# Rounding weights in a casting transfer and forming their rests in an adding transfer

## The chip, the cores and the metric

The kernel runs on one core of a Trainium2 chip. The metric is the device time of one execution in microseconds. Times inside an execution are counted from the start of its profiled span.

## What is computed

One layer of a decoder step for 576 tokens: 512 of a prompt and 64 of eight sampled sequences (8 each), with 16 learned tokens ahead of the prompt in the recurrent and attention branches. An input projection feeds two branches, a state-space scan and a sparse attention. Their outputs go through two projections, are weighted by gates and added, and then come the two parts that this document is about, cut to their core:

```
merged = sigmoid(g_ssm) * (y_ssm @ w_ssm_proj) + sigmoid(g_attn) * (y_att @ w_attn_proj)
h  = h + merged @ w_out                                  # w_out: 1024 x 1024
u2 = rmsnorm(h, norm2_w)
h  = h + square(relu(u2 @ w_up)) @ w_down                # w_up: 1024 x 4096, w_down: 4096 x 1024
y  = rmsnorm(h, final_norm_w)
```

All arrays are float32.

## The kernel before

**Two-part numbers.** TensorE runs in a format of fewer mantissa bits (`float32r`, FR in the code). To keep precision, an operand x is held as two tiles: hi, which is x rounded to that format, and lo = x - hi, the rest. A product of two such operands is three matmuls: hi*hi, hi*lo and lo*hi. The 64 sample tokens put their own hi and lo side by side in one tile, so that for them two matmuls do the work of three.

**Weights.** `weights` (from L125 on) loads a raw weight tile of 128 x 1024 into `wr` (two buffers for the whole kernel) by transfers that SyncE (SP) issues, and `split` (L122, L123) makes the two parts: ScalarE (ACT) writes hi from raw (L122), VectorE (DVE) writes lo = raw - hi (L123). Most weights go to the tiles `wh` and `wl` (three buffers each). The weights of the output projection `w_out` and of the lower projection `w_down` are taken by rows through `row_weights` (L1089) and go to `dh` and `dl`, seven buffers each, in the pool `p4w`. There are 40 such tiles of 512 KB: 8 of `w_out` and 32 of `w_down`.

**The output projection.** The five token blocks are taken in the order 4, 0, 1, 2, 3; block 4 is the 64 sample tokens, whose operand tile also holds their rests. `add_product` multiplies one block by four weight tiles and adds the result to `h2`. For each of the two column halves (512 wide) it collects the products of the four weight tiles in one PSUM accumulator: 12 matmuls for a prompt block, 8 for block 4 (L1177). VectorE then adds the accumulator to `h2` (L1179). The 1024 rows of `w_out` are done in two halves, four weight tiles each. Accumulators come from the groups "s" and "a", three of each. Before the first of them, the attention projection (matmuls at L145 into the accumulators "w") is finished. After the second half the second norm follows: squares on ScalarE (L1113), a power on GpSimd (POOL, L155), a scaling on VectorE, and transposes on TensorE (L1135).

**The MLP.** The 4096 hidden columns are cut into eight blocks of 512. For block s, `ups` makes four up projections (matmuls at L145 into "a"), and `add_product` multiplies the result by the four `w_down` tiles of the block, here with the accumulators "s" alone. The loop runs one block ahead: the up projections of block s + 1 are traced before the lower projection of block s, and the `w_down` tiles of block s between them:

```
    for s in range(8):
        ws = [] if s < 7 else row_weights(a["w_down"][0], 512 * s, 4)
        nxt = ups(s + 1, ws) if s < 7 else None
```

At block 7 there is no up projection left: its lower projection follows that of block 6 directly. The final norm and the stores come last.

**Order.** The program is traced in the order of the code. The framework's planner then sets the order of instructions on each engine, by estimates of its own of when operands and buffers are ready, and puts in the semaphores. Work from further down the code is thus moved forward where an engine would be idle. Each engine executes its own list strictly in order: an instruction that waits holds up all that stand behind it on that engine, transfers that the engine issues included. A tile whose slot is still read waits for its last reader.

Of the kernel before, what the change touches and what calls it, by code (L numbers as in the profile page):

```python
# [9 lines left out]
FT = mybir.dt.float32  # L10
FR = mybir.dt.float32r
BF = mybir.dt.bfloat16
I32 = mybir.dt.int32
AF = mybir.ActivationFunctionType
OP = mybir.AluOpType
# [55 lines left out]
def body(ctx, tc, a, o):  # L71
    nc = tc.nc
    SB, PS, DR = bass.MemoryType.SB, bass.MemoryType.PSUM, bass.MemoryType.DRAM
    act, dve, pool, pe, sy = nc.scalar, nc.vector, nc.gpsimd, nc.tensor, nc.sync
# [33 lines left out]
    def flat(t):  # L108
        return t.rearrange("p a b -> p (a b)")
# [11 lines left out]
    def split(raw, hi, lo, lo_eng=None):  # L121
        act.activation(hi, raw, AF.Copy)  # L122
        (lo_eng or dve).tensor_tensor(lo, raw, hi.bitcast(FT), op=OP.subtract)  # L123

    def weights(parts, at=None, lo_eng=None):  # L125
        raw = wp.tile([128, 8, 128], FT, tag="wr", name="wr", bufs=WB[0])
        lo, hi = [(at[0] if at else wp).tile([128, 8, 128], FR, tag=n, name=n, bufs=at[2] if at else WB[1])
                  for n in (at[1] if at else ("wl", "wh"))]
        for sel, src in parts:
            sy.dma_start(sel(raw), src)  # L130
        split(raw, hi, lo, lo_eng)
        return hi, lo

    def block(src, r0, c0, kt=8):
# [2 lines left out]
    def whole(src, r0, c0):  # L137
        return weights([(lambda r: r, block(src, r0, c0))])
# [45 lines left out]
    for t in range(5):  # L184
        xt = p0.tile([128, D], FT, tag="xt", name="xt", bufs=5)
        load_x(t, xt)
        if t == 4:
            sy.dma_start(xt[64:80], meta)
        if t == 2:
            w0 = weights([(lambda r: r[:, :, 0:96], w_in[:, C_KI:C_KI + 96].rearrange("(k p) c -> p k c", p=128)),  # L190
                          (lambda r: r[:, :, 96:128], w_in[:, C_DT:C_DT + 32].rearrange("(k p) c -> p k c", p=128))], lo_eng=dve)
        if t == 0:
            sy.dma_start(cst[0], a["cst"][:, 0:KEPT])
            sy.dma_start(wrow, rows(a["norm1_w"], D))
        xts.append(xt)
    ssq = p0.tile([128, 5], FT, name="ssq1")
    rs = p0.tile([128, 5], FT, name="rs1")
    for t in range(5):
        n = 128 if t < 4 else 80
# [6 lines left out]
        for q in range(2):  # L206
            ps = mis()
            pv = ps.rearrange("p (k n) -> p k n", k=4)
            for i in range(4):
                k = 4 * q + i  # L210
                pe.transpose(pv[:, i, :n], xn[:n, 128 * k:128 * k + 128], idf[:n, :n])
            h_ = uh[:, 4 * q:4 * q + 4, 128 * t:128 * t + n]
            act.activation(h_, pv[:, :, :n], AF.Copy)
            dve.tensor_tensor(ul[:, 4 * q:4 * q + 4, 128 * t:128 * t + n], pv[:, :, :n], h_.bitcast(FT), op=OP.subtract)  # L214
    wq0 = weights([(lambda r: r, block(w_in, 0, C_QI))])

    cwr = p0.tile([128, 128], FT, name="cwr")
# [70 lines left out]
    with tc.tile_pool(name="p1", bufs=1) as p1:  # L288
# [76 lines left out]
        for b2 in range(2):  # L365
            for e in range(2):
                src = qis[64 * e:64 * e + 64].rearrange("p c (i b s) -> p b i c s", b=2, s=8)[:, b2]
# [49 lines left out]
        for t in range(4):  # L417
            at = am[:, LO[t]:LO[t] + LT[t]]
# [82 lines left out]
        for kt in range(6):  # L501
            c0, n = ((128 * kt, 128) if kt < 4 else (512, 16) if kt == 4 else (528, 64))
# [515 lines left out]
    for q in range(4):  # L1018
# [7 lines left out]
        for m in range(8):  # L1026
            if m % 2 == 0:
                src = w_s[512 * q:512 * q + 512, 128 * m:128 * m + 256].rearrange("(k p) c -> p k c", p=128)
# [29 lines left out]
    for m in range(8):  # L1058
        parts = []
        for e in range(2):  # L1060
            for hp in range(2):
                r0 = 64 * (8 * hp + 4 * e)
# [25 lines left out]

    def row_weights(src, r0, n, at=(p4w, ("dl", "dh"), 7)):  # L1089

        return [[flat(x) for x in weights([(flat, src[r0 + 128 * k:r0 + 128 * k + 128, :])], at)] for k in range(n)]

    wo = row_weights(a["w_out"][0], 0, 4)
    def norm_rows(name):
        row = p4.tile([128, D], FT, tag="wrow", name="wrow", bufs=1)
# [87 lines left out]
    for q in range(2):  # L1183
        ws = row_weights(a["w_out"][0], 512, 4) if q else wo
        for t in ORDER:
            add_product(t, [mgh[:, 4 * q + k, :] for k in range(4)], [mgl[:, 4 * q + k, :] for k in range(4)], ws, banks="sa")
            if q == 1:
                turns.append(norm2(t))
                if t in (0, 1, 2):
                    turns.pop(0)()  # L1190
# [15 lines left out]
    def ups(s, ws=None):  # L1206
        hh = [p5.tile([128, NQ + NS], FR, tag="hh", name="hh", bufs=9) for _ in range(4)]
        hl = [p5.tile([128, NP], FR, tag="hl", name="hl", bufs=9) for _ in range(4)]

        def w_up(f):  # L1210
            return whole(a["w_up"][0], 0, 512 * s + 128 * f)

        f0 = 0
        if s == 0:
            f0 = 3
            w3 = [w_up(f) for f in range(3)]
            for c in PARTS:
                for f in range(3):
                    up(w3[f], f, hh, hl, *c)
                    if turns:  # L1220
                        turns.pop(0)()
        for f in range(f0, 4):
            w = w_up(f)
            for c in HALVES:
                up(w, f, hh, hl, *c)
            if ws is not None:
                ws += row_weights(a["w_down"][0], 512 * (s - 1) + 128 * f, 1)
        return hh, hl
# [36 lines left out]
```

## Time and profile before

| | us |
|---|---|
| median of 3 runs (1493.74 to 1494.7) | 1494.07 |
| the profiled execution | 1499.61 |
| its span, first to last instruction | 1497.8 |
| TensorE busy | 1443.2 (96%) |
| VectorE busy | 973.9 (65%) |
| ScalarE busy | 695.1 (46%) |
| GpSimd busy | 324.1 (22%) |
| 40 rounding passes on `dh`, ScalarE | 42.5 |
| 40 subtractions into `dl`, VectorE | 49.0 |

The profiled execution is 5.5 us longer than the median of the runs without a profile. Busy time counts the instructions of an engine and not the issuing of transfers; the ends of matmuls are modelled, since they overlap. In a row of a timeline the first number is the start in us, the second the length. In a row of a tile the three numbers are the least, the median and the greatest length in ns, then come the first and the last start. "x40" is a count. "SPq" and "POOLq" are the queues of SyncE and GpSimd. What stands in brackets behind a row of a timeline is the idle time ahead of it on its engine and what ended it.

### The profile page before, as it was taken

How to read it: one execution, taken by the hardware profiler on the slowest of the kernel's cores; microseconds unless marked ns; L12 is line 12 of the kernel's file. 1: busy time of each engine (PE TensorE's matmuls, PEld its weight loads, DVE VectorE, ACT ScalarE, POOL GpSimd, SP SyncE). 2: the span in 40 equal slices, each digit the busy share in tenths (PEclk: the TensorE clock that was granted, in tenths of full speed). 3: DMA queues.
4: the chain of work that ended last, by engine and by line, in shares of the span. 5: the costliest groups of instructions: out<-in, count | busy, mean ns of one | idle time of the engine just before them, and what ended most of it. 6: DMA issues, size and time to landing. Idle time of an engine off the chain costs nothing.

```text
span 1497.8 us, 26553 instructions
## 1 busy us (share of the span) xinstructions
PE 1443.2 (96%) x9960; PEld 1293.7 (86%) x9960; DVE 973.9 (65%) x2010; ACT 695.1 (46%) x1548; POOL 324.1 (22%) x475
## 2 busy tenths in 40 slices
PE   6899999999999999999999999999999999999998
PEld 5899989987888888889688888898898998899886
DVE  5599989998868767582644777665654444444434
ACT  4454255546665654542655777732352331232211
POOL 1100011426636335342423633100000000000001
PEclk9899999999999999999999999999999999999999
DMA  6334365768897887878964532146143321231202
GB/s 178 107 66 118 115 173 167 208 195 220 231 263 201 255 221 197 247 198 252 293 228 142 155 87 79 43 129 194 50 133 93 99 85 57 85 112 58 84 28 70
DMA packets 297609, 221.54 MB, mean 148 GB/s; under 512 B 43821, under 2 KB 267361, under 8 KB 297457
## 3 DMA queue, kind: packets, MB, share of 16 engines
q1 hardware_dynamic: 292232, 200.98, 47.5%
q0 software_dynamic: 5248, 18.88, 3.7%
q8 instruction: 78, 1.28, 0.4%
q14 instruction: 51, 0.41, 0.1%
HBM read 174.97 MB, written 44.07 MB: 146 GB/s over the span
## 4 chain that ended last, share of the span: by engine, by line
PE 76%; DMA 11%; DVE 5%; ACT 2%; issue 2%; SPq 1%; POOL 1%; POOLq 0%; DVEq 0%; ACTq 0%
PE w L145 22%; PE s L1177 16%; PE a L145 14%; PE w L1039 7%; PE s L871 2%; PE a L1177 2%; PE s L1005 2%; DMA out_dram<-st 1%; DMA bc<-d_ac 1%; DMA wr<-in_w_ssm_proj_dram 1%; DMA st<-in_state_ssm_dram 1%; PE s L734 1%; PE a L894 1%; PE a L995 1%; DMA d_x<-tk 1%
## 5 line engine op out<-in xcount | busy, mean ns | idle before, releaser
L145 PE MATMUL w<-uh,wh 128*128 128x288 f32 (+1 forms) x1168 | 359.1, 307 | 12.8 <-DVE qS L322 4.3
L145 PE MATMUL w<-uh,wl 128*128 128x288 f32 (+1 forms) x1168 | 354.9, 304 | 0.0
L145 PE MATMUL w<-ul,wh 128*128 128x288 f32 (+1 forms) x1168 | 352.6, 302 | 0.6 <-DVE ul L214 0.6
L145 PEld LDWEIGHTS w<-uh,wh 128*128 128x128 f32 x1168 | 223.6, 191 | 20.5 <-issue 7.1
L123 DVE TENSOR_TENSOR wl<-wr,wh 128x1024 fp32r<-128x1024 f32 x129 | 161.1, 1249 | 117.1 <-ACT wh L122 114.9
L145 PEld LDWEIGHTS w<-ul,wh 128*128 128x128 f32 x1168 | 223.5, 191 | 3.9 <-issue 2.3
L145 PEld LDWEIGHTS w<-uh,wl 128*128 128x128 f32 x1168 | 222.4, 190 | 1.5 <-issue 0.8
L122 ACT ACTIVATE wh<-wr 128x1024 fp32r<-128x1024 f32 x129 | 136.3, 1056 | 147.5 <-PE w L145 84.5
L145 PE MATMUL a<-u2h,wh 128*128 128x288 f32 (+2 forms) x512 | 151.4, 296 | 0.0
L145 PE MATMUL a<-u2l,wh 128*128 128x288 f32 (+2 forms) x512 | 151.2, 295 | 0.0
L145 PE MATMUL a<-u2h,wl 128*128 128x288 f32 (+2 forms) x512 | 151.2, 295 | 0.0
L1177 PE MATMUL s<-dl,hh 128*128 128x512 f32 (+1 forms) x324 | 126.9, 392 | 0.0
L1177 PE MATMUL s<-dh,hh 128*128 128x512 f32 (+1 forms) x324 | 126.8, 392 | 0.0
L1179 DVE TENSOR_TENSOR h<-h,s 128x512 f32<-128x512 f32 (+1 forms) x91 | 61.2, 679 | 100.4 <-PE s L1177 100.3
L122 ACT ACTIVATE dh<-wr 128x1024 fp32r<-128x1024 f32 x40 | 42.5, 1062 | 178.1 <-PE s L1177 138.3
L155 POOL TENSOR_TENSOR rs<-rs,cst 128x1 f32<-128x1 f32 (+2 forms) x15 | 8.3, 552 | 446.0 <-DVE rs L154 445.9
L1177 PE MATMUL s<-dh,hl 128*128 128x512 f32 (+1 forms) x260 | 101.7, 391 | 0.0
L145 PEld LDWEIGHTS a<-u2l,wh 128*128 128x128 f32 x512 | 96.1, 188 | 0.6
L145 PEld LDWEIGHTS a<-u2h,wh 128*128 128x128 f32 x512 | 96.1, 188 | 0.6
L145 PEld LDWEIGHTS a<-u2h,wl 128*128 128x128 f32 x512 | 96.1, 188 | 0.0
L1039 PE MATMUL w<-ysh,wh 128*128 128x288 f32 x256 | 78.4, 308 | 0.2 <-DVE ms L1044 0.2
L123 DVE TENSOR_TENSOR dl<-wr,dh 128x1024 fp32r<-128x1024 f32 x40 | 49.0, 1225 | 45.3 <-ACT dh L122 45.2
(384 smaller groups left out, 3220.1 us busy)
## 6 DMA issues: line engine op xcount, KB each, us to landing
wr<-in_w_in_dram SPq DMA_DIRECT2D x64, 512.0 KB
wr<-in_w_up_dram SPq DMA_DIRECT2D x32, 512.0 KB
wr<-in_w_down_dram SPq DMA_DIRECT2D x32, 512.0 KB
st<-in_state_ssm_dram SPq DMA_DIRECT2D x16, 512.0 KB
bc<-d_ac SPq DMA_DIRECT2D x32, 256.0 KB
out_dram<-st SPq DMA_DIRECT2D x16, 512.0 KB
wr<-in_w_ssm_proj_dram SPq DMA_DIRECT2D x16, 512.0 KB
d_xd<-th SPq DMA_DIRECT2D x16, 296.0 KB
```

The source lines that it names most:

```text
L122: act.activation(hi, raw, AF.Copy)
L123: (lo_eng or dve).tensor_tensor(lo, raw, hi.bitcast(FT), op=OP.subtract)
L145: pe.matmul(ps[:, :c1 - c0], p[:, k, :], x[:, c0:c1], start=(k == 0 and i == 0), stop=(k == 7 and i == 2))
L155: pool.tensor_tensor(dst, dst, K("half")[:p, :cols], op=OP.pow)
L734: pe.matmul(py[64 * (hh % 2):64 * (hh % 2) + 64, 128 * (hh // 2):128 * (hh // 2) + n], xt[:n, 64 * hh:64 * hh + 64], mt, start=True, stop= ...
L871: pe.matmul(v[64 * hp:64 * hp + 64], QZ[:, hp, :], kk, start=True, stop=True)
L894: pe.matmul(py[h, 0:128], PTs[:, s, h], Vg[s // 4][:, 256 * (s % 4) + 128 * hp:256 * (s % 4) + 128 * hp + 128], start=(s == 0), stop=False)
L995: pe.transpose(pv[:, j, :], P2[:, e, 128 * j:128 * j + 128], idf)
L1005: pe.matmul(py[64 * e:64 * e + 64, 0:256], Vt[:, j, kv:kv + 64], PT[:, e, j], start=(j == 0), stop=False)
L1039: pe.matmul(ps[:, :HQ], p[:, k, mc], x[k][:, c0:c1], start=(k == 0 and i == 0), stop=(k == 3 and i == 2))
L1177: pe.matmul(ps, x, w[:, cc], start=(k == 0 and i == 0), stop=(k == len(ws) - 1 and i == len(terms) - 1))
L1179: dve.tensor_tensor(h2[:, t, cc], h2[:, t, cc], ps, op=OP.add)
```

## The change

For the 40 tiles of `dh` and `dl`, the raw tile, its load by SyncE and the subtraction on VectorE go. A new function takes their place:

```
+    def weights_by_dma(src, at, view):
+
+        lo, hi = [at[0].tile([128, 8, 128], FR, tag=n, name=n, bufs=at[2]) for n in at[1]]
+        pool.dma_start(out=view(hi), in_=src)
+        act.activation(lo, hi.bitcast(FT), AF.Copy, scale=-1.0)
+        pool.dma_start(out=view(lo), in_=src, accum_op=OP.add)
+        return hi, lo
...
     def row_weights(src, r0, n, at=(p4w, ("dl", "dh"), 7)):
 
-        return [[flat(x) for x in weights([(flat, src[r0 + 128 * k:r0 + 128 * k + 128, :])], at)] for k in range(n)]
+        return [[flat(x) for x in weights_by_dma(src[r0 + 128 * k:r0 + 128 * k + 128, :], at, flat)] for k in range(n)]
```

The first transfer reads the weights in float32 and writes hi in the format of TensorE. ScalarE writes -hi into lo. The second transfer reads the same weights again and adds them to lo, which then holds the weights less hi. GpSimd issues both transfers. The number of buffers, the matmuls and all other weights (`w_in`, `w_ssm_proj`, `w_attn_proj`, `w_up`) stay as they are.

## The prediction

> **What bounds the kernel now.** I read the page's head first, then a table of busy time by stage, then the chain that ended last, then the rows of the two tiles that the change rewrites.
>
> ```profile
> PE 1443.2 (96%) x9960; PEld 1293.7 (86%) x9960; DVE 973.9 (65%) x2010; ACT 695.1 (46%) x1548; POOL 324.1 (22%) x475
> ...
> PEclk9899999999999999999999999999999999999999
> ```
>
> ```profile
> core 0: us, PE busy (x) PEld busy (x) DVE busy (x) ACT busy (x) POOL busy (x), PEclk, DMA share, GB/s
> 975.00:1024.00 49.00, 49.00 (x357) 48.33 (x358) 32.09 (x62) 18.27 (x26) 0.47 (x1) 0.95 0.50 149
> 1024.00:1081.00 57.00, 57.00 (x283) 47.00 (x282) 32.96 (x50) 14.78 (x25) 4.21 (x7) 0.95 0.35 107
> ...
> 1128.00:1440.00 312.00, 312.00 (x1834) 281.02 (x1833) 140.34 (x234) 87.50 (x149) 0.00 (x0) 1.00 0.27 82
> 1440.00:1460.00 20.00, 20.00 (x87) 16.05 (x87) 5.93 (x10) 0.07 (x1) 0.00 (x0) 1.00 0.00 0
> ...
> 1488.00:1498.00 10.00, 2.85 (x25) 2.65 (x23) 4.90 (x9) 1.74 (x6) 3.66 (x5) 0.78 0.27 105
> ```
>
> ```profile
> 1128.36 6.52 PE s L1177 x28
> 1134.88 0.80 PE a L145 x6
> 1135.67 19.59 PE s L1177 x84
> 1155.26 24.80 PE a L145 x186
> ...
> 1438.60 49.47 PE s L1177 x212
> 1488.06 0.02 issue
> ```
>
> TensorE is busy in every microsecond of the stages that the change touches: 49.00 of 49.00, 57.00 of 57.00, 312.00 of 312.00. The chain says the same: from 1128.36 to 1488.06 it is matmuls and nothing else. One step of the loop over the hidden blocks is 6.52 + 0.80 + 19.59 + 24.80 = 51.7 us. A 512-wide matmul comes every 19.59 / 84 = 0.2333 us, and no stage in the chain shows a gap that a faster producer could close. VectorE and ScalarE are near half idle there (140.34 and 87.50 of 312.00), GpSimd and most of the DMA engines wholly or nearly so. So time can be lost in these stages, but hardly won.
>
> **What is removed.** The rows of tile dh and of its raw buffer wr:
>
> ```profile
> L122 ACT ACTIVATE dh<-wr x40: 1046/1062/1067, 1000.9 to 1462.4; 128x1024 fp32r<-128x1024 f32 x40
> L123 DVE TENSOR_TENSOR dl<-wr,dh x40: 1218/1225/1227, 1002.0 to 1463.5; 128x1024 fp32r<-128x1024 f32 x40
> L130 SPq DMA_DIRECT2D wr<-in_w_down_dram x32: 327/328/340, 1091.6 to 1425.6; - x32
> L130 SPq DMA_DIRECT2D wr<-in_w_out_dram x8: 327/328/339, 997.3 to 1021.9; - x8
> ```
>
> 40 subtractions of 1.225 us leave VectorE: 49.0 us of busy time. None lies on the chain, so the gain is 0. 40 issues of 0.33 us leave SyncE: 13 us, also off the chain, gain 0. ScalarE still passes over each tile once (now it writes the negated rounded tile instead of the rounded one), 40 x 1.062 us as before, change 0. The two-slot raw buffer wr now serves the up projection alone, so those loads start sooner. No matmul waits for them today, so that too is 0. What covers all of this is the full TensorE; it goes only if a new stall opens.
>
> **What is added.** Two GpSimd transfers for each of 40 tiles. No casting or adding transfer is in this trace. The nearest rows are the gathers that GpSimd issues, in 512 KB (Kg, Vg: 128 rows of 4 KB, as a weight tile has) and 256 KB (kr):
>
> ```profile
> L385 POOL DMA_INDIRECT kr<-in_cache_kidx_dram,idx x8: 942/978/1175, 35.3 to 109.8; - x8
> ...
> DMA to landing us min/median/max: 3.3/3.5/6.7
> ...
> L850 POOL DMA_INDIRECT Kg<-in_cache_k_dram,idx x16: 934/938/1761, 687.8 to 771.6; - x16
> ...
> DMA to landing us min/median/max: 4.4/6.3/15.9
> ...
> L850 POOL DMA_INDIRECT Vg<-in_cache_v_dram,idx x16: 932/937/1517, 690.4 to 805.8; - x16
> ...
> DMA to landing us min/median/max: 4.3/4.6/4.9
> ```
>
> Issue: 80 x 0.94 = 75 us of GpSimd, in some 500 us in which it does almost nothing. Hidden. Landing of the casting transfer: 4.3 to 6.3 us; I take 4.6 (Vg's median: where it counts, from 1440 on, the DMA engines are at 0.00). The adding transfer must also read the tile it adds to. kr against Vg gives (4.3 - 3.3) = 1.0 us for 256 KB more, so 512 KB more are 2.0 us: an estimate of 6.6 us, with 4.3 (the extra read is free) and 8.3 (Kg's median plus 2.0) as ends. Whether adding itself runs slower than copying, no row shows; that is a rival below.
>
> So the way from a free slot to a finished rest changes from 1.06 + 1.23 = 2.3 us (the raw tile lay waiting in wr) to 4.6 + 1.06 + 6.6 = 12.3 us. What counts is where this way is not started early enough. Seven slots serve dh and dl, four tiles make a step. The first three tiles of a step take slots free for a whole step; the fourth takes the slot of the first tile of the step before, free only in that step's last group of twelve matmuls. For the hidden blocks 0 to 6 the fourth tile then has the 24.80 us of up-projection matmuls ahead of it: slack 24.8 - 12.3 = 12 us, cost 0. Twice there is no such cover.
>
> **Place one, the last step (block 7).**
>
> ```profile
> 1392.52 33.41 SPq L130 DMA_DIRECT2D wr<-in_w_down_dram  x5
> ```
>
> ```profile
> 1462.42 1.06 ACT L122 ACTIVATE dh<-wr 128x1024 fp32r<-128x1024 f32 x1 [22.35 <-PE s L1177]
> ```
>
> ```profile
> 1461.99 0.40 PE L1177 MATMUL s<-dh,hl 128*128 128x512 f32 x1
> ...
> 1464.55 0.39 PE L1177 MATMUL s<-dh,hh 128*128 128x512 f32 x1
> ...
> 1466.18 0.40 PE L1177 MATMUL s<-dl,hh 128*128 128x512 f32 x1
> ```
>
> The last raw tile is issued by 1425.9 (1392.52 + 33.41) and lies ready; its split starts at 1462.42, right after the matmul that frees the slot (1461.99 + 0.40 = 1462.39). Step 7 begins at 1464.55, and its eighth matmul, at 1466.18, is the first to want the fourth rest. After the change the transfer can start only at 1462.39: rounded tile at 1467.0, negated at 1468.1, rest at 1474.7. What TensorE can do meanwhile: three accumulators of the group "s" can hold the first three weight tiles of token block 4 (two halves, 6 matmuls each) and of half a block 0 (9): 21 x 0.2333 = 4.9 us, then the four products with the rounded fourth tile, 0.9 us. That ends at 1470.4. Stall: 4.3 us. Ends: 1.7 us (4.3 + 1.06 + 4.3), and 7.7 us (6.3 + 1.06 + 8.3). If the order of TensorE stays as it is, the wait starts at 1466.18 and costs 8.5 us with the middle values. I take 4.3, because the order is written by a planner that fills such a wait, as the next rows show.
>
> **Place two, the second half of the output projection.**
>
> ```profile
> 1044.01 0.40 PE L1177 MATMUL s<-dh,mgl 128*128 128x512 f32 x1
> ...
> 1046.57 0.39 PE L1177 MATMUL a<-dh,mgh 128*128 128x512 f32 x1
> ...
> 1051.47 0.40 PE L1177 MATMUL s<-dl,mgh 128*128 128x512 f32 x1
> ```
>
> Eight tiles share seven slots; the eighth waits for the first, free at 1044.01 + 0.40 = 1044.41. In group "s" its rest is used at 1051.47. In plain order (8 matmuls in "a", then 8 in "s") that would be the sixteenth from 1046.57, at 1046.57 + 15 x 0.2333 = 1050.07: the planner put six other products in front. New finish: 1044.41 + 12.3 = 1056.7. Six accumulators are in use here ("s" and "a"), with room for 12 + 4 x 9 = 48 matmuls, 11.2 us, to 1057.8. Stall 0 with a full refill, 5.2 us with today's order (1056.7 - 1051.47); I take 0.6, as the planner's own figure for these transfers is not visible.
>
> **GpSimd's queue.** The adding transfer waits, at the head of GpSimd's queue, for ScalarE, which waits for the casting one. Behind it can stand the powers of the second norm:
>
> ```profile
> 1059.15 0.57 POOL L155 TENSOR_TENSOR rs<-rs,cst 64x1 f32<-64x1 f32 x1 [1.67 <-DVE rs L154]
> ```
>
> Five of them feed the token blocks that TensorE needs from 1064 on, and the first w_down tiles take their slots in just this stretch. One wait costs between 0 and 4.6 us; other matmuls cover most. I take 0.5. Sum: +4.3 + 0.6 + 0.5 = +5.4 us.
>
> The profiled execution took 1499.61 us with a span of 1497.8; the sum puts that span at 1503.2. The runs without the profile have a median of 1494.07, and a stall is the same there: 1494.07 + 5.4 = 1499.5 us.
>
> **Rule against row.** The Trainium skill, "DMA: Bandwidth & Descriptors", section "Anatomy of one DMA — SWDGE (gpsimd) path", prices a GpSimd transfer at 2.0 us plus its bytes at 436 GB/s: an estimate of 3.2 us for 512 KB, where this trace has 4.3 at the least. By it the last rest would be there at 1469.9 and the stall of place one would be zero. The same page's "Rules for kernel authors" says that an adding transfer reads its destination and writes it later; that speaks for a price above Vg's, but no run so far shows one.
>
> **Rivals.** *Hidden (not slower).* The planner sets other work before the fourth tile, or the landings are short. For: it did so at 1046 to 1051. Against: with the least landing of the rows, 4.3 us, and a full refill there is still 1.7 us of stall. It decides where the way from slot to rest falls under 1470.4 - 1462.4 = 8.0 us. Time: 1494 to 1496.5, say 1495. The page's 3.2 us is this case. Chance 0.27.
>
> *Order unchanged, or a slow adder.* The planner reckons the transfers too short: 8.5 + 5.2 + 0.5 = +14.2 us, 1508. An adding transfer of 12 us does about as much (+5.4 at each place). For: nothing here prices it. Chance 0.18.
>
> *The DMA engines become the bound from 975 to 1024.*
>
> ```profile
> 690.00:740.00 50.00, 46.48 (x333) 37.04 (x333) 20.88 (x43) 24.61 (x54) 15.68 (x16) 0.92 0.92 299
> ```
>
> Seven w_out tiles would move 1.0 to 1.5 MB each instead of 0.5: with 149 GB/s over 49 us that makes some 11 to 14.5 MB, 220 to 300 GB/s, as much as in the one stage that is full (0.92), where TensorE lost 50.00 - 46.48 = 3.5 us. Against: the loads can spread, and the attention weights are fetched a step ahead. +9 us with the stalls above, 1503. Chance 0.05.
>
> *Faster.* Less VectorE work might raise the granted clock of 0.95 before 1128. Against: at 0.95 a 512-wide matmul comes every (1046.57 - 1044.01) / 11 = 0.233 us, at 1.00 every 0.2333, so the clock is not what sets the pace, and over 3 us is hardly possible. 1490.5. Chance 0.03.
>
> **How the numbers follow.** The forecast (4 to 6 us of stall, 1497 to 1502) has 0.47. A measurement tells 0.2% from no change, 3.0 us here: 1491.1 to 1497.1. Hidden lies in it whole, and 0.05 of the forecast: same 0.32. Faster 0.03. Slower 0.42 + 0.18 + 0.05 = 0.65. The range takes in hidden, the order unchanged and a rather slow adder, 1493 to 1510; outside are the faster case and the worst adders, some 0.13.
>
> **What will show it.** Right: TensorE idle of 2 to 8 us between 1462 and 1478, put down to a DMA on dl or to ScalarE; GpSimd rows of some 0.94 us, 80 of them; landings of 4.5 us for dh and 6 to 7 for dl; VectorE 49 us less busy, SyncE without w_down. Wrong: TensorE full to the end (hidden), idle in each 51.7 us step (slow adder), or idle before 1024 (DMA). A rewritten order of the query stage before 975, since GpSimd and ScalarE have work there too, would make all of this beside the point.

## The result and the profile after

| | before | after |
|---|---|---|
| median | 1493.9 us (1492.65 to 1494.7, 4 runs) | 1513.76 us (1510.26 to 1519.93, 4 runs) |
| profiled execution, span | 1497.8 us | 1517.9 us |
| TensorE busy | 1443.2 us | 1446.8 us |
| VectorE busy | 973.9 us | 930.4 us |

The ratio of the runs is 1.0142, 95% interval 1.0112 to 1.0172; by the medians the change costs 19.9 us. The forecast was 1499.5 us, the range ended at 1510. The direction was right, the size was not. All line numbers from the new function on are 8 higher: the product is now at L1185, its addition to h2 at L1187, the norm's transposes at L1143; the casting transfer is L137, the negation L138, the adding transfer L139. In the experiments the numbers are up to four higher still.

The stages of the prediction's table, in the changed kernel. The columns are those shown there: the length of the stage, busy time and count of TensorE, weight loads, VectorE, ScalarE and GpSimd, granted clock, share of the DMA engines, GB/s.

```profile
975.00:1024.00 49.00, 42.40 (x279) 39.91 (x279) 20.27 (x44) 16.57 (x24) 6.38 (x8) 0.93 0.85 207
1024.00:1081.00 57.00, 52.92 (x273) 44.64 (x271) 25.66 (x45) 13.29 (x19) 8.69 (x12) 1.00 0.58 162
...
1128.00:1440.00 312.00, 312.00 (x1840) 281.28 (x1839) 112.51 (x205) 85.28 (x145) 33.86 (x48) 1.00 0.47 117
...
1460.00:1488.00 28.00, 25.14 (x108) 19.87 (x106) 5.26 (x8) 1.06 (x1) 1.41 (x2) 1.00 0.18 38
```

TensorE was full in all of these. Now it lacks 6.6 us in the first, 4.1 in the second, 2.9 in the last, while the long loop is as full as before, with VectorE down from 140.34 to 112.51. The changed kernel's waits of TensorE after 960 us give the places, with the sum, the count and the longest of each:

```profile
PE a L1185 <- issue: 5.4, 1, 5.4
PE s L1185 <- DMA dl<-in_w_down_dram: 3.1, 1, 3.1
PE w L1143 <- DVE xn L1131: 2.1, 1, 2.1
PE a L1143 <- DVE xn L1131: 2.0, 1, 2.0
PE w L153 <- DVE tga L1080: 1.2, 1, 1.2
```

**The burst, 968 to 1005 us.** Seven casting transfers leave GpSimd at 968.78 and 974.18, seven adding ones between 978.71 and 994.19. Busy time in slices of 10 us, first the changed kernel, then the kernel before:

```profile
970.00:980.00 10.00, 9.23 (x67) 7.96 (x66) 5.52 (x12) 4.83 (x8) 3.86 (x7) 1.00 1.07 367
980.00:990.00 10.00, 10.00 (x72) 9.70 (x71) 3.12 (x6) 5.63 (x7) 4.00 (x5) 1.00 1.06 226
990.00:1000.00 10.00, 8.23 (x55) 7.25 (x53) 2.11 (x5) 1.40 (x2) 0.87 (x1) 1.00 1.07 214
1000.00:1010.00 10.00, 5.16 (x14) 4.14 (x15) 5.34 (x11) 3.15 (x5) 0.00 (x0) 0.66 0.96 215
```

```profile
980.00:990.00 10.00, 10.00 (x77) 10.00 (x76) 5.76 (x13) 3.81 (x6) 0.00 (x0) 0.95 0.57 161
990.00:1000.00 10.00, 10.00 (x77) 10.00 (x76) 6.43 (x14) 2.50 (x5) 0.00 (x0) 0.95 0.45 130
```

The DMA engines are full for 40 us (a share a little above 1 stands for full). While the casting transfers run they move 367 GB/s, while the adding ones run about 215. In the same stretch SyncE has to bring the attention weights and the gate rows `tga`. It issues them as early as before; changed kernel first, then before:

```profile
979.57 0.49 SPq L1075 DMA_DIRECT2D tga<-d_g  x1
980.10 4.90 SPq L130 DMA_DIRECT2D wr<-in_w_attn_proj_dram  x3
...
985.92 19.00 SPq L130 DMA_DIRECT2D wr<-in_w_attn_proj_dram  x4
```

```profile
979.65 0.49 SPq L1067 DMA_DIRECT2D tga<-d_g  x1
980.18 4.90 SPq L130 DMA_DIRECT2D wr<-in_w_attn_proj_dram  x3
...
985.77 5.71 SPq L130 DMA_DIRECT2D wr<-in_w_attn_proj_dram  x4
```

But they land late. By the semaphore updates in the trace, the gate rows issued at 979.57 landed at 991.43 (before: 979.65 and 983.04), and the last piece of an attention tile, issued at 980.74, landed at 1001.84, after 21.1 us (before: 980.83 and 984.18, 3.4 us). The 19.00 us of the next four issues are a sign of the same: two of them take 3.82 and 5.46 us instead of 0.62 and 0.60, and the last one waits for the buffer that the late tile holds. TensorE waits for the late landings, not for these four issues. The timeline of the changed kernel shows who waits, in the bracket at the end of each row:

```profile
991.52 0.46 DVE L1080 SCALAR_TENSOR_TENSOR tga<-tga,w 128x288 f32<-128x288 f32 x1 [6.57 <-DMA tga<-d_g]
...
1001.99 1.06 ACT L122 ACTIVATE wh<-wr 128x1024 fp32r<-128x1024 f32 x1 [8.09 <-issue]
...
1004.84 0.76 PE L1185 MATMUL a<-dh,mgh 128*128 128x512 f32 x1 [5.45 <-issue]
```

VectorE waits 6.57 us for the gate rows. ScalarE waits 8.09 us for the late attention tile; its split stood at 988.54 before. The rounding of merged rows stands behind that split in ScalarE's list, so the next products with merged rows are late too. TensorE, which had brought w_out products forward meanwhile, runs dry at 999.39. After the restart at 1004.84 it has a granted clock of 0.50 until 1009, which is the 0.66 of the last slice.

**The second norm, 1076 to 1081 us.** Block 4 is the first to be normed, and its 64-row transfer into `other` comes before everything else:

```profile
1053.64 0.55 POOL L137 DMA_DIRECT2D dh<-in_w_out_dram  x1 [16.02 <-PE s L1185]
1054.34 0.54 POOL L137 DMA_DIRECT2D dh<-in_w_down_dram  x1
1055.04 0.53 POOL L137 DMA_DIRECT2D dh<-in_w_down_dram  x1 [0.16 <-PE s L1185]
1055.73 0.53 POOL L137 DMA_DIRECT2D dh<-in_w_down_dram  x1 [0.17 <-PE s L1185]
1058.98 0.89 POOL L139 DMA_DIRECT2D dl<-in_w_out_dram  x1 [2.72 <-ACT dl L138]
...
1069.19 0.52 SPq L1118 DMA_DIRECT2D other<-h  x1
1073.75 1.22 DVE L1119 TENSOR_TENSOR h<-h,other 64x1024 f32<-64x1024 f32 x1 [2.24 <-DMA other<-h]
...
1078.35 0.71 PE L1143 MATMUL w<-cst,xn 64*128 64x64 f32 x8 [2.15 <-DVE xn L1131]
```

The eighth w_out tile gets its slot at 1053.64, three w_down casting transfers go out before its adding one, and block 4 is done only near 1069. From there to the first transpose it is a serial chain of 9.2 us (1069.19 to 1078.35), and the products that TensorE had left for it ended at 1076.2. Behind the two waits the granted clock is 0.50 from 1081 to 1084. The three casting transfers did not hold up the adding one in GpSimd's queue: GpSimd was idle for 2.72 us ahead of it, until ScalarE had negated the tile.

**Block 7.** This is place one of the prediction:

```profile
1477.28 0.55 POOL L137 DMA_DIRECT2D dh<-in_w_down_dram  x1 [39.25 <-PE s L1185]
...
1481.26 1.06 ACT L138 ACTIVATE dl<-dh 128x1024 fp32r<-128x1024 f32 x1 [26.59 <-DMA dh<-in_w_down_dram]
...
1482.61 0.86 POOL L139 DMA_DIRECT2D dl<-in_w_down_dram  x1 [4.78 <-ACT dl L138]
...
1488.24 0.94 PE L1185 MATMUL s<-dl,hh 128*128 128x512 f32 x3 [3.11 <-DMA dl<-in_w_down_dram]
...
1491.12 0.63 PE L1185 MATMUL s<-dl,hh 128*128 128x512 f32 x1
1491.54 0.63 PE L1185 MATMUL s<-dh,hh 128*128 128x512 f32 x1
...
1493.94 0.40 PE L1185 MATMUL s<-dh,hh 128*128 128x512 f32 x1
1494.17 0.40 PE L1185 MATMUL s<-dh,hl 128*128 128x512 f32 x1
```

From the free slot to the first product with the rest it takes 11.0 us. TensorE has other work for 7.9 us of it (it runs dry at 1485.14). The last rows show a cost behind the stall: for eight matmuls the pitch is 0.42 us (1491.12 to 1491.54) instead of 0.23 (1493.94 to 1494.17), 1.5 us in all. It is the granted clock, which falls to 0.50 some 2 us after the restart:

```profile
1491.00:1492.00 1.00, 1.00 (x4) 0.71 (x4) 0.00 (x0) 0.00 (x0) 0.00 (x0) 0.50 0.81 176
```

**The account.** One number per stretch is less noisy than the whole time: O runs from the first matmul of the attention projection to the first one of the up projection, M from there to the last hi*hi one of the lower projection. Ahead of O even the old kernel differs from execution to execution: in two profiles of it, on one chip, O began at 934.1 and at 944.2 us, while O and M agreed within 0.3 us. All values in us, from the starts of those matmuls:

| kernel | O | M | time against its own before |
|---|---|---|---|
| before | 132.4 | 415.0 | |
| after | 146.5 | 420.5 | 1.0142 [1.0112, 1.0172] |
| e0, e9 all old | 131.5, 131.7 | 415.4, 415.1 | 1.0016 [0.9992, 1.0041], 1.0003 [0.998, 1.0025] |
| e1, e8 w_down only | 132.8, 139.0 | 420.4, 421.0 | 1.0111 [1.0092, 1.0129], 1.0074 [1.0049, 1.01] |
| e2 w_out only | 140.4 | 415.0 | 1.0106 [1.0083, 1.0129] |
| e3 second transfer copies | 136.9 | 417.2 | 1.0073 [1.0047, 1.01] |
| e4 two tiles old | 140.7 | 415.0 | 1.0105 [1.0081, 1.0129] |
| e5 31 w_down tiles only | 132.4 | 415.0 | 1.0026 [0.9999, 1.0052] |
| e6 paced | 150.0 | 421.5 | 1.0203 [1.0186, 1.022] |
| e7 paced, two tiles old | 145.1 | 415.2 | 1.0117 [1.0094, 1.014] |
| e10 eight slots | 139.9 | 415.1 | 1.0052 [1.0025, 1.008] |
| e11 three w_out tiles | 135.3 | 415.0 | 1.002 [0.9996, 1.0044] |
| e12 old, eight slots | 133.3 | 415.0 | 1.0016 [0.9995, 1.0038] |
| e13 w_down, eight slots | 132.5 | 415.1 | 1.0014 [0.9991, 1.0037] |
| e14 copies, eight slots | 134.0 | 415.3 | 1.0037 [1.0011, 1.0064] |

The change added 14.1 us to O and 5.5 to M, 19.6 together, which is the 19.9 of the times. O's part splits, by e2 and e4, into some 8 us of burst and 6 of second norm. The waits shown make 10.7 of the 14.1 and 3.1 of the 5.5 us. Most of the difference is the half clock behind them: TensorE ran at 0.50 from 1004.84 to 1009 and from 1081 to 1084, and half of that is 3.6 us (an estimate); in M it is the 1.5 us above. Some 0.9 us of M remain, 0.3 of them a short wait for an addition to h.

### The profile page after: what moved, and what is told of

It reads as the page before. It is cut to its first block, busy times and chain, and to the rows that moved or that the text cites. A ratio compares the mean times of both kernels' runs of the same rounds, so it can differ in the third digit from the quotient of the medians.

```text
span 1517.9 us, 26584 instructions
## 1 busy us (share of the span) xinstructions
PE 1446.8 (95%) x9960; PEld 1296.5 (85%) x9960; DVE 930.4 (61%) x1970; ACT 694.3 (46%) x1548; POOL 380.6 (25%) x555
## 4 chain that ended last, share of the span: by engine, by line
PE 51%; issue 25%; DMA 13%; DVE 4%; POOL 3%; ACT 3%; SPq 1%; POOLq 0%; ACTq 0%; DVEq 0%
PE w L153 23%; PE w L1047 7%; PE s L1185 3%; DMA dh<-in_w_down_dram 2%; PE s L1013 2%; DMA bc<-d_ac 2%; POOL dl L139 2%; PE a L1185 1%; DMA wr<-in_w_ssm_proj_dram 1%; PE s L742 1%; PE s L879 1%; PE a L1003 1%; DMA xt<-d_x 1%; PE a L902 1%; PE s L754 1%
## 5 line engine op out<-in xcount | busy, mean ns | idle before, releaser
L153 PEld LDWEIGHTS w<-uh,wh 128*128 128x128 f32 x1168 | 223.3, 191 | 19.9 <-issue 8.4
L1187 DVE TENSOR_TENSOR h<-h,s 128x512 f32<-128x512 f32 (+1 forms) x91 | 61.5, 680 | 142.1 <-PE s L1185 141.4
L138 ACT ACTIVATE dl<-dh 128x1024 fp32r<-128x1024 f32 x40 | 42.0, 1056 | 206.3 <-DMA dh<-in_w_down_dram 186.4
L1185 PE MATMUL s<-dl,hh 128*128 128x512 f32 (+1 forms) x324 | 127.3, 394 | 3.1 <-DMA dl<-in_w_down_dram 3.1
L1185 PE MATMUL s<-dh,hh 128*128 128x512 f32 (+1 forms) x324 | 127.4, 394 | 0.3 <-DVE h L1187 0.3
L1185 PE MATMUL s<-dh,hl 128*128 128x512 f32 (+1 forms) x260 | 102.4, 394 | 0.0
L137 POOL DMA_DIRECT2D dh<-in_w_down_dram x32 | 17.3, 541 | 318.0 <-PE s L1185 308.7
L1047 PE MATMUL w<-ysh,wl 128*128 128x288 f32 x256 | 76.7, 300 | 0.0
```

The costliest lines, as they stand in the source:

```text
L137: pool.dma_start(out=view(hi), in_=src)
L138: act.activation(lo, hi.bitcast(FT), AF.Copy, scale=-1.0)
L153: pe.matmul(ps[:, :c1 - c0], p[:, k, :], x[:, c0:c1], start=(k == 0 and i == 0), stop=(k == 7 and i == 2))
L1047: pe.matmul(ps[:, :HQ], p[:, k, mc], x[k][:, c0:c1], start=(k == 0 and i == 0), stop=(k == 3 and i == 2))
L1185: pe.matmul(ps, x, w[:, cc], start=(k == 0 and i == 0), stop=(k == len(ws) - 1 and i == len(terms) - 1))
L1187: dve.tensor_tensor(h2[:, t, cc], h2[:, t, cc], ps, op=OP.add)
```

## The experiments

**e0 and e9, all old.** `row_weights` as before, the new function present and unused.

> The kernel before with the new function in the file but not called, for a trace on the chip of the other runs. All theories: the time of the kernel before, ratio 0.999 to 1.001.

> The old loading for all 40 tiles with the new function present and unused, profiled beside the kernel above on the same chip: the yardstick for where time goes. Same time as the kernel before within 0.3%, a stretch of 547 us from the start of the attention projection to the end of the last lower product, no idle time of TensorE over 0.5 us in it. Rival P is borne out only if its attention projection starts over 2 us earlier than that of the kernel with new w_down tiles.

Same time as before, both times. The two profiles are the yardstick for O and M.

**e1 and e8, w_down alone.** w_out goes through `weights` as before:

```
-    wo = row_weights(a["w_out"][0], 0, 4)
+    wo = row_weights(a["w_out"][0], 0, 4, old=range(4))
...
-        ws = row_weights(a["w_out"][0], 512, 4) if q else wo
+        ws = row_weights(a["w_out"][0], 512, 4, old=range(4)) if q else wo
```

> The 8 tiles of w_out are loaded and split as before; the 32 tiles of w_down go through the casting and the adding transfer. Theory A (most of the loss is a burst of GpSimd transfers for w_out that fills the DMA engines from 970 to 1010 and delays the attention weights, then the second norm is late; block 7 costs the rest): only block 7's 5 us are left, about 1499 us, ratio 1.002 to 1.005, TensorE idle only near the last block. Rival B (the adding transfers cost something in every step): over 1503 us, with idle TensorE in the steps before block 7.

> Once more the kernel in which only the 32 w_down tiles come by the two GpSimd transfers and w_out is loaded as before: a second profiled execution, to see where the time goes that the first one did not show (about +6 us in the traced stretch from the attention projection to the last product, against +14.6 us in the times). Theory S (the stall at the last hidden block is the loss, and its length varies with the landing of the adding transfer): this execution shows one stall of 3 to 12 us ahead of the last block, nothing over 0.5 us elsewhere after 940 us, and the stretch from the attention projection to the last lower product takes 547 + 1.5 + that stall. Rival P (the loss lies ahead of the changed tiles, in the first 940 us, which the change does not touch): the attention projection starts over 2 us later than in the old kernel run beside it, and the stretch itself is longer by no more than 6 us. Time 1503 to 1508 either way.

M is longer by 5 to 6 us in both: place one. In the traced execution of e1 that is all. Yet its time, 1505.66 us, is above the 1499 of theory A and in the range of rival B, whose idle time in the steps before block 7 the trace does not show; the difference stays open (see below). The traced execution of e8 has another stall, in the second norm. Waits of TensorE in e8:

```profile
PE w L1144 <- DVE xn L1132: 3.7, 1, 3.7
PE s L1186 <- DMA dl<-in_w_down_dram: 2.8, 1, 2.8
```

So in this execution the loss does not lie in the untouched first part (P falls: O begins at 931.2 here, earlier than in either old profile), and the stalls vary between executions of one kernel. Behind each of the two stalls the granted clock is 0.50 for some 6 us, against some 3 us behind the stall of e1, so O and M grow by more than the waits. S is right on block 7 and wrong in that nothing else would stall; the time, 1501.38 us, is below what both named. The timeline of e8 shows what the norm waited for:

```profile
1041.09 0.52 SPq L1119 DMA_DIRECT2D other<-h  x1
...
1053.78 1.22 DVE L1120 TENSOR_TENSOR h<-h,other 64x1024 f32<-64x1024 f32 x1 [8.92 <-DMA other<-h]
```

From issue to use 12.7 us, where the same pair stands 3.5 us apart before (1053.02 and 1056.49). Three adding transfers of w_down are issued within 4 us around it. In e1 the distance is 7.6 us, in e5 7.7, in e13 6.3: late each time, and covered each time but this.

**e2, w_out alone.** `old=range(4)` at the two w_down calls instead.

> The opposite: the 8 tiles of w_out go through the two transfers, the 32 of w_down are loaded and split as before. Theory A: the loss of the w_out stretch stays, 9 to 16 us, about 1506 us, ratio 1.006 to 1.011, with TensorE idle between 990 and 1005 and before the second norm's transposes, and none at block 7. Rival C (the prediction's own: only the wait for the slot of the last tile costs, once per matrix): about 1495 us, ratio under 1.002.

O +8.0, M unchanged: the whole burst, with the 5.4 us wait, and 0.8 us in the second norm. Rival C, with 1495 us, falls. Without the w_down transfers behind the eighth w_out tile the second norm hardly stalls: the tile's adding transfer lands after 5.5 us instead of 6.4, and `other` is used 3.0 us after its issue instead of 4.6. In O and M the two halves do not add up to the change: 8.0 in e2 and 5.8 in e1 make 13.8 of the 19.6 us. The 6 us of the second norm need both halves, or an execution like that of e8, which stalls there without the new w_out tiles.

**e3, the second transfer copies.** The rest tile then holds the weights themselves, so the low part of these products is not the reference's:

```
-        pool.dma_start(out=view(lo), in_=src, accum_op=OP.add)
+        pool.dma_start(out=view(lo), in_=src)
```

> Both transfers stay, but the second one copies instead of adding (so the rest tile holds the whole weights, and the output is another one). Theory D (adding is slow in the DMA engines: they are over 0.95 busy at some 215 GB/s while it runs): the burst after 970 is over sooner, landing of the second transfer falls from 8.4 us (median) to about 5, TensorE's idle time before 1010 falls from 6.6 us to under 3, and the time to 1500 to 1506 us. Rival E (the number and the size of the transfers matter, whatever they do): 1510 to 1516 us, idle time as with adding.

Its traffic is counted in the same bytes. In e3 the slices from 970 to 990 move over 320 GB/s, and the engines are done by 1000:

```profile
970.00:980.00 10.00, 10.00 (x75) 10.00 (x76) 7.34 (x16) 7.85 (x11) 2.48 (x5) 1.00 1.16 331
980.00:990.00 10.00, 9.21 (x62) 8.42 (x61) 2.25 (x7) 2.88 (x4) 1.66 (x4) 1.00 1.24 326
```

The waits before 1010 fall from 6.6 us to 2.2, that ahead of block 7 from 3.1 to 1.4. The adding is the larger part of the cost, as theory D has it. Of the two waits in the second norm the first falls from 2.1 to 0.6, the second stays at 2.0.

**e4, old handover.** The eighth w_out tile and the last w_down tile, which wait for a slot, are loaded as before (`old=(3,)` at the second w_out call and at block 7).

> Only the eighth tile of w_out and the last tile of w_down, the two that wait for a slot with nothing to cover them, are loaded and split as before; the other 38 go through the two transfers. Theory A: block 7's 5 us go, and the 5 us at the second norm go too if the late eighth tile is what delays block 4 there; the 8 us before 1010 stay: about 1502 us, ratio 1.004 to 1.007. Rival C (the slot wait is all): 1494 to 1496 us. If the second norm stays late all the same: about 1507 us.

M is back at 415.0 and the norm no longer stalls; the burst stays (waits of 5.4 and 1.3 us). So the burst and the two handovers are separate losses. The time, 1504.02 us, is above the 1502 of theory A.

**e5, the hidden tiles.** Only the 31 w_down tiles that have cover, all else old.

> Only the 31 tiles of w_down that have a full step of matmuls ahead of them go through the two transfers; the 8 tiles of w_out and the last tile of w_down are loaded and split as before. Theory A (all loss is stalls at the w_out burst, the second norm and block 7): the time of the kernel before, ratio 0.998 to 1.002, which would also show that 31 x 1.23 us taken off VectorE win nothing. Rival B (each transfer by GpSimd costs something that the stalls do not show, because the runs of the variant with w_down alone are 14 us over the kernel before while its traced stalls make 6): ratio 1.005 to 1.008.

O and M are those of the kernel before (132.4 and 415.0), and O is not shorter than in the two old profiles, although VectorE has 31 subtractions less: nothing is won by freeing it. The timed ratio, 1.0026, is just above what theory A allowed and far from rival B; its interval includes 1 at its edge.

**e6 and e7, paced.** A copy of eight columns on GpSimd, reading the merged rows of step k, is put ahead of the casting transfer of tile k, for the first seven w_out tiles, so that the transfers spread over the attention projection; e7 also has the two tiles of e4 old:

```
+        if gate is not None:
+            pool.tensor_copy(view(hi)[:, 0:8], gate)
         pool.dma_start(out=view(hi), in_=src)
```

> The changed kernel, but the first seven casting transfers of w_out are released one by one: GpSimd first copies 8 columns of the merged branch output of tile k into weight tile k, so the transfer of tile k waits for step k of the attention projection (about 6.4 us apart) instead of all seven starting at 969. Theory A: the DMA engines are no longer full from 970 to 1010, the attention weights come in time, TensorE's 6.6 us of idle time before 1005 go, and 8 us of the loss; about 1505 us, ratio 1.005 to 1.010. Rival F (the total of the bytes counts, not the burst): no better than the changed kernel, 1.012 to 1.016.

> As the paced one, and in addition the eighth tile of w_out and the last tile of w_down are loaded and split as before. Theory A: every traced stall is gone, ratio 0.999 to 1.003. Rival B: 1.006 to 1.010, with TensorE full and the loss outside its stalls.

Pacing did not help; e6 is the slowest kernel of all. Both times are above what either theory named (1.0203 against 1.016 at the most, 1.0117 against 1.010). The DMA engines stay near full, for longer (shares of 0.77 to 1.14 from 970 to 1030). A slice of e6 and its waits:

```profile
980.00:990.00 10.00, 8.46 (x62) 8.02 (x60) 3.77 (x8) 1.39 (x2) 1.92 (x3) 1.00 1.12 248
```

```profile
PE w L155 <- DVE tga L1082: 7.6, 4, 4.1
```

TensorE waits for what the gate rows feed four times, and the w_out products, which had filled TensorE, cannot start before 1022.5. e7 has the same loss in the burst (8.7 us of such waits) and, with its two tiles old, none behind it. That the transfers go out at once is thus not the whole cause, as theory A had it. This speaks for F, the engine time that they take beside the attention loads. It does not prove F: the paced kernels also get their w_out tiles later, so TensorE has nothing to bring forward.

**e10, eight slots.** Eight buffers for dh and dl instead of seven, so that no fourth or eighth tile waits for a slot; hh and hl give a buffer each to make room (eight instead of nine). **e12** is the old kernel with these sizes, **e13** w_down alone with them.

> All 40 tiles by the two transfers, but eight slots for dh and dl instead of seven, so that the fourth tile of a step takes a slot that has been free for a step and the eighth w_out tile waits for nobody (paid for by eight instead of nine buffers for hh and hl). Theory S (place one and place two are waits for a slot): the stall ahead of the last hidden block and the 4 us of idle time in the second norm go, the idle time of 5 to 8 us between 985 and 1010 us stays or grows a little (eight tiles in the burst instead of seven): 1502 to 1506, as with the old handover of those two tiles. Rival (the two transfers are late in themselves, however early the slot is free): the last block still stalls over 2 us and the time stays above 1508.

> The kernel before with eight slots for dh and dl and eight buffers for hh and hl: what these sizes do by themselves, the yardstick for the kernels with eight slots. Both theories: no change, 0.997 to 1.003, a stretch of 547 us from the attention projection to the last lower product. If it is slower by 2 us or more, that much of the loss of the eight-slot kernels is not the transfers'.

> Only the 32 w_down tiles by the two transfers, with eight slots. Theory S (of the w_down tiles only the wait for a slot costs time): no idle time over 0.6 us after 940 us, a stretch of 547 to 548 us, ratio 0.998 to 1.004. Rival (the traffic of 32 casting and adding transfers beside the up weights costs TensorE something by itself): the stretch is 550 us or more although no slot is waited for, ratio 1.005 or more.

The one long wait left in e10 is the burst's:

```profile
PE w L153 <- DVE tga L1080: 5.4, 1, 5.4
```

M is 415.1 with all 32 w_down tiles by the two transfers, and 415.1 in e13: of the w_down tiles only the wait for a slot costs time in M. e13 cannot be told from before, and e12 neither. O of e10 is 6.6 us above that of e12, and its time of 1500.61 us a little below the 1502 to 1506 of S.

**e11, three tiles.** Only the first three w_out tiles by the two transfers.

> Only the first three w_out tiles by the two transfers, the other five and all of w_down as before: the dose of the burst cut from eight tiles to three. Theory A (the adding transfers fill the DMA engines while the attention weights are to be loaded, and the stall is what the queue behind them is late beyond its slack): three tiles of 0.5 MB occupy the engines for under 10 us, less than the load of the attention weights is ahead, so no stall or one under 1.5 us, and 1490 to 1495. Rival Q (GpSimd's issue or any single adding transfer is what delays the attention weights): the stall of 5.4 us of the eight-tile dose stays at over 3 us, and 1500 to 1505.

One wait of 2.0 us, put down to tga; ahead of it ScalarE had waited 6.59 us for an attention weight load, whose split held up the rest. O is 3.6 us above the old profile of the same round; behind the wait the granted clock was 0.50 for some 3 us, which makes an estimated 1.6 of them. It lies between the two expectations (under 1.5, over 3); three tiles already outrun the slack that the attention loads have, and more tiles cost more. The time itself is within what can be told from no change.

**e14, copies and eight slots.** e3's edit with the sizes of e10; the low part is again not the reference's.

> All 40 tiles by two transfers with eight slots, the second of them copying instead of adding (the rest tile then holds the weight itself, so the low part of these products is not computed rightly): the burst before 1010 us without its adding, and with no slot waits elsewhere. Theory D (it is the adding that fills the engines): the DMA engines move over 300 GB/s from 970 to 990 and are done before 1000, idle time of TensorE there under 2.5 us against 5.4 with adding, stretch 548 to 551 us, ratio 1.000 to 1.004. Rival (the second reading of the weights, the sheer bytes, fills them): idle time of over 4 us and a ratio above 1.005, as with adding.

This is the pair for e10: same slots, same bytes, no adding. The longest wait in the burst falls from 5.4 to 1.6 us:

```profile
PE w L153 <- DVE tga L1080: 1.6, 1, 1.6
```

O is 0.7 us above e12 instead of 6.6. So the adding makes some 6 of the 6.6 us; 0.7 is left for the second reading, beyond what the slack of the loads hides. The engines did stay full past 990 us (a share of 1.05 from 990 to 1000), longer than expected.

What adding costs the engines can be read off the long loop, where nothing waits. The stage from 1128 to 1440 us holds 24 tiles (48 issues of GpSimd). GpSimd's queue there (packets, MB, share of the 16 engines), in e14 and in e10:

```profile
q0 software_dynamic: 6912, 25.17, 25.2%
```

```profile
q0 software_dynamic: 6912, 25.17, 34.2%
```

Packets and bytes are the same, and the share of the engines is 9.0% higher when the second transfer adds: (34.2 - 25.2)% x 312 / 24 = 1.2 us of all 16 engines more per tile. If a casting transfer takes as long as a copying one, which no run separates, each takes 25.2% x 312 / 48 = 1.6 us and an adding one 2.8 us, some 1.7 times a copy (an estimate). In the burst of the changed kernel, with the engines full, the seven adding transfers land 2.4 to 3.2 us after one another. What takes the extra time is not in the counted bytes.

No kernel here beats the old one. Where nothing waits, the change gains nothing, since TensorE was full.

## Why the prediction went wrong

**Right.** TensorE bounds these stages; VectorE's time and SyncE's issues are worth nothing here (31 subtractions less in e5, 32 in e13, no gain). The hidden w_down tiles cost nothing: the chain of the changed kernel shows a step's transfer at the same distance as before, 51.7 us, each landing in some 4 us:

```profile
1219.53 3.85 DMA dh<-in_w_down_dram
...
1271.24 4.03 DMA dh<-in_w_down_dram
...
1477.28 3.87 DMA dh<-in_w_down_dram
1482.61 5.50 DMA dl<-in_w_down_dram
```

**Place one: 4.3 us forecast, 5.5 measured (M).** The way from slot to rest was put at 12.3 us and took 11.0: by the last two rows above, the casting transfer 3.87 for 4.6, the adding one 5.50 for 6.6. That is the quiet price; the rows of tile dl in the changed kernel have a median of 8.4 and up to 14.2:

```profile
L139 POOL DMA_DIRECT2D dl<-in_w_down_dram x32: 856/873/1252, 1060.3 to 1482.6; - x32
L139 POOL DMA_DIRECT2D dl<-in_w_out_dram x8: 863/874/915, 978.7 to 1059.0; - x8
...
DMA to landing us min/median/max: 5.4/8.4/14.2
```

GpSimd's issues were put at 0.94 us and take 0.87 (adding) and some 0.55 (casting). The cover was put at 8.0 us and was 7.9 (1477.28 to 1485.14). So the stall was 3.1 us and not 4.3, and what the sum lacked is the slow restart, 1.5 us: that the total came near is in part luck. The granted clock was not looked for behind a stall: 0.66 from 1000 to 1010. The Trainium skill, "TensorE: Matmul & The Clock Gate", Part 1, gives half the clock after an idle window of about 3.4 us, and 426.7 ns from one 512-wide matmul to the next. The granted 0.50 and the 0.42 us here agree; the idle time before them was shorter here, 3.1 us at block 7 and 2.0 us in e11.

**Place two and GpSimd's queue: 0.6 + 0.5 us forecast, 6 measured.** This is one of the two steps that failed. It asked only when TensorE would want the eighth rest, and the planner did fill that wait. It did not follow what block 4's late end releases: the transfer into `other`, the norm and the transposes, a chain for which only the products put off before it were left as cover. The way from slot to rest was right: 12.3 us forecast, 11.8 measured (slot at 1053.64, adding transfer issued at 1058.98, landed after 6.4 us). GpSimd's queue held up nothing here; what the w_down transfers cost on this path is the later landing of the rest and of `other`, 2.5 us by the comparison with e2.

**The DMA engines from 975 to 1024: chance 0.05, but it was the largest term, 8 us.** This is the other failed step. The mechanism was named, its price (3.5 us, taken from the gather stage) and the reason against it were not right: "the loads can spread" reckoned bytes over 49 us, 220 to 300 GB/s. But an adding transfer holds the engines some 1.7 times as long as a copy of the same bytes, so from 980 to 1000 the engines were full at 214 to 226 GB/s (a share of 0.85 at 207 GB/s over the whole stage). And all seven slots were free ahead of it, so the planner sent all seven tiles at once; the attention weights, "fetched a step ahead", were split 13.5 us late (1001.99 - 988.54) and cost 6.6 us of waits, so that about 7 us were covered, while the engines were full for 40. The half clock behind the waits adds some 2 us. Idle time before 1024 was one of the prediction's own signs of being wrong. The row that would have told is in the prediction's own stage table: a share of 0.50 at 149 GB/s before. The 4.2 MB of w_out are over half of the 7.3 MB there, so a doubled or tripled w_out load takes the share to some 0.8 to 1.1 (an estimate).

The rivals "hidden" and "faster" are refuted. "Slow adder" was right in its premise and wrong in the place: ahead of block 7 the adding took 5.50 us, not 12; its slowness counted through the full engines.

**Open.** On the chip of e1 to e4 the timed loss is some 5 to 9 us more than O and M of the profiled execution show (e2: 1506.29 against 1491.05, +15.2, with O and M +8.0). e8 shows that a second execution of the same kernel can have a stall that the first had not; whether that is the whole of it is not shown, since no old kernel was profiled beside those four. Neither O nor M holds the tail behind the last matmul, which is 7.2 to 7.7 us in most profiles and 8.5 to 9.0 in e1, e2, e5, e8 and e13; why is not known. The link of the late gate rows and attention weights to the full engines is read from the traces and from e3, e11 and e14; no kernel moved the attention loads themselves.

## What to carry to other kernels

Price an adding transfer by the engine time it takes, here about 1.7 copies of its bytes, and compare the sum with the free share of the engines in each stage where its slots fall free, not over the whole kernel. Then look at which small loads on the path (here gate rows, 256 KB of h, a weight tile with one step of slack) share the engines with it. Add the slow restart behind a stall, here 1.5 to 3 us. When a transfer moves behind the release of a buffer, follow the released work to the end of its chain: the wait may fall where the next stage begins, not where the operand is read.

## What the runs showed of the hardware

Adding transfers of 512 KB, all in flight together, keep the share of the DMA engines at 1.0 while only 214 to 226 GB/s are counted; casting ones move 367 and copying ones 326. By itself, an adding transfer landed in 5.50 us, a casting one in 3.87. Adding took the engines 1.2 us more per 512 KB than copying, with the same counted bytes. A small load of SyncE in the same stretch landed after 21.1 us instead of 3.4, and two of SyncE's issues took 3.82 and 5.46 us instead of some 0.6. Behind stalls of TensorE of 2.0 us (e11) to 5.4 us the granted clock was 0.50 for some 3 us, in e8 for some 6, and 512-wide matmuls came at 0.42 us instead of 0.23; behind stalls of 1.4 us and one of 2.0 us in e3 it stayed at 1.00. The drop can come late: 2 us after the restart in block 7.
